# Four modulation blocks of layer 2: from TensorE products in layer 1 to VectorE multiply-adds in the scans of layer 2

## The chip, the cores and the metric

The kernel runs on one core of a Trainium2 chip. The metric is the device time of one execution in microseconds (us), lower is better. TensorE is called PE in the profile (PEld is its loading of weights), VectorE is DVE, ScalarE is ACT, GpSimd is POOL, and SyncE, which issues nearly all transfers here, is SP.

## The reference

The model is a trunk of two layers over 256 latent tokens (x) with 256 context tokens (ctx) ahead of them, 2048 features wide. Layer 1 mixes by attention (neighbourhood attention and latent attention, eight heads each). Layer 2 mixes by a gated delta rule, scanned in both directions over chunks of 64 tokens. Each layer is modulated by a conditioning vector, one for the latent tokens (c) and one for the context tokens (c_ctx):

```
def adaln_params(cond, w_mod, b_mod):
    return jnp.split(jax.nn.silu(cond) @ w_mod + b_mod, 3, axis=-1)

def deltanet_layer(x, ctx, c, c_ctx, w_mod, b_mod, norm, w_in, ..., update_ctx):
    sh, sc, gt = adaln_params(c, w_mod, b_mod)
    sh_c, sc_c, gt_c = adaln_params(c_ctx, w_mod, b_mod)
    ... modulate(x, norm, sh, sc) @ w_in ... modulate(ctx, norm, sh_c, sc_c) @ w_in ...
    x = x + gt[:, None] * deltanet_out(o_xf + flip_t(o_xb), zx, o_norm, w_out)
    if update_ctx:
        ctx = ctx + gt_c * deltanet_out(o_cf + flip_t(o_cb), zc, o_norm, w_out)
    return x, ctx
```

In layer 2, the last one, update_ctx is false. So its gate gt is needed for the latent tokens only, and only at the very end, when the output product is added to x. Shift and scale are needed for both, at the layer's beginning.

## The kernel before, in words

Everything lies feature-major: 128 features on the partitions, 16 tiles of them, and the 512 tokens (256 latent, 256 context) along the free axis. Dense products split each fp32 operand into a high and a low part of a shorter format and add three products (lines 90 to 92). A weight tile of 128 x 1024 is loaded into one of four buffers called raw, cast to its high part by ScalarE (whi) and subtracted by VectorE (wlo).

**Modulation.** The weights of a layer's modulation are 2048 x 6144. They are worked in 12 chunks of 512 columns, each 4 MB in 8 loads of 512 KB: chunks 0 to 3 are the shift, 4 to 7 the scale, 8 to 11 the gate. There are two ways to work a chunk. `adaln` (from line 121) does it on TensorE: 16 products of cond (the two samples, padded to 32 columns) with a 128 x 512 piece of weights, spread over four column groups of the array, into the tile pmod; VectorE copies that to macc; four transposes bring it to the partitions (pmt); VectorE adds the four groups and the bias into mods. A profile records each of these fp32 products as two instructions. `adaln_lanes` (from line 161) does it on VectorE: for each of 16 weight rows and each of the two samples one multiply-add `acc = raw * cond + acc` over 128 x 512 (line 177), and at the end eight products with a column of ones (line 184, tile pml) that sum over the partitions.

**Layer 1** works, in this order, the gate projection, the heads of the neighbourhood attention, the latent heads, the output product with `ab_wo`, and the norm and modulation of layer 2's input (`modulate`, lines 229 to 243, which makes the tiles hx, high and low, 16 feature tiles one after another on VectorE, ScalarE and GpSimd). The order of instructions on each engine is set there by a planner that runs the program in a simulated timeline and puts instructions where they become ready by it. Layer 2's modulation is mixed into layer 1 by generators. Chunks 0 and 1 are lanes in the neighbourhood heads. Chunks 2, 3 and 8 are products in the latent heads: `later(mr, ((1, (2, 3, 8), 0),))`, one quarter of a chunk per head, the rest after the last head. Chunk 9 follows as products behind the last head, chunks 4 to 7 are lanes in the output product, and chunks 10 and 11 are products during the norm and `modulate`. In the latent heads q's rotated part (qr) lies in a buffer that the split of the attention's output (gx, lines 502 and 503) takes over when qr has been read. cond lies with the activations of layer 1 in a pool (abx) whose space layer 2's constants (taps, ad, line 540) and pools take over.

**Layer 2** first projects gates, keys, queries, and inverts the small matrices of the delta rule. Then come the scans: a loop over steps `st` from -2 to 69, in which the order on TensorE, VectorE and ScalarE is the written order (`manual_schedule`); SP's order stays with the planner. A step is a quarter of a head. It holds a step of the context's scan C for head st // 4 and, six steps later, one of the latent tokens' scan X; in each, TensorE multiplies the state (pks, line 1033), VectorE makes R (line 1037), TensorE multiplies R into ptr (line 1045), ScalarE and VectorE split that (vh, vl), TensorE updates the state's product (line 1064) and VectorE the state (line 1073), and X ends with a product and a subtraction (lines 1078, 1083). Between these phases stand eight pieces of a value projection for later heads (`take(dn, ...)`), which keep TensorE busy, and the convolution of the values, whose taps (line 585) stand on VectorE at the middle and the end of even steps. A finished head is normed and gated (`finish`; its last instruction on VectorE, re, line 1111, ends a step with st % 4 = 0). `hi()` casts the next weight tile at the start of a step and loads ahead, so that three tiles are loaded and not yet cast; `lo()` makes the low part in the second half. From step 58 the value projection is replaced by the output product, whose `project` (line 636) reads the gate, `mods[1][:, 32 + u, 0:1]`, sample 0 alone.

`room["e"]` is a buffer of 4096 columns that the scans cut up; its last 1024 columns (`tail_e`) are used from step 56 on, for rows of the gated output read back by `gate`.

Of the kernel before, what the change touches and what calls it, by code (L numbers as in the profile page):

```python
# [16 lines left out]
KT = 16  # L17
# [9 lines left out]
def trunk_kernel(ctx: ExitStack, tc: tile.TileContext, g):  # L27
# [35 lines left out]
    ab_bmod, dn_bmod = vecs[:, 56:104], vecs[:, 104:152]  # L63
    o_gain = vecs[:, 152:153]
    mods = [cst(f"mod{l}", [128, 48, 2]) for l in range(2)]
    Am = [cst(f"Am{l}", [128, KT, 2]) for l in range(2)]


# [92 lines left out]
    def adaln_lanes(l, ps, pm, tp, chunks, after=None):  # L161

        wm, bmod, gain = ((g["ab_wm"], ab_bmod, ab_gain), (g["dn_wm"], dn_bmod, dn_gain))[l]
        for ch in chunks:
# [26 lines left out]
                V.tensor_tensor(Am[l][:, f], Am[l][:, f], gain[:, f].unsqueeze(2).broadcast_to([128, 4, 2]), op=ALU.mult)  # L191
            yield

    def steps(it, n=1000):
        for _ in range(n):
            if next(it, it) is it:
                break
# [62 lines left out]
    with tc.tile_pool(name="s0", bufs=2) as tp, tc.tile_pool(name="s0p", bufs=1, space=PSUM) as ps:  # L260
        V.memset(cond, 0.0)
        A.activation(cond[:, :, 0:2], cc, AF.Silu)
        xs = ((xA, g["xT"]), (xB, g["cT"]))
        for j in range(0, KT, 4):
            for x, src in xs:
                nc.sync.dma_start(x[:, j:j + 4], src[:, j:j + 4])

        xq = tp.tile([128, 6, 4, S], F32, name="xq", tag="zs", bufs=1)
        sums = [xq[:, 0], xq[:, 1]]
        for j in range(0, KT, 4):  # L270
            for i, (x, _) in enumerate(xs):
                sq = xq[:, i if j == 0 else 2 + (j // 2 + i) % 4]
                A.activation(sq, x[:, j:j + 4], AF.Square)
                if j > 0:
                    V.tensor_tensor(sums[i], sums[i], sq, op=ALU.add)
        for t in sums:
            V.tensor_tensor(t[:, 0:2], t[:, 0:2], t[:, 2:4], op=ALU.add)
            V.tensor_tensor(t[:, 0], t[:, 0], t[:, 1], op=ALU.add)
        rb = rstd_bcast([b for t in sums for b in blocks_of(t[:, 0], n=S)], 4, D, ps, "pz3", tp)
        rbs = tp.tile([128, T], F32, name="rbs", tag="rbs", bufs=1)  # L280
        V.tensor_copy(rbs, rb)
        pz = [ps.tile([128, T], F32, name=f"pz{i}", tag=f"pz{i}") for i in range(NP)]
        zs = tp.tile([128, NS - NP, T], F32, name="zs", tag="zs", bufs=1)

        GROUPS = [(0, 1), (1, 1), (2, 2),(4,2),(6,2), (8, 4), (12, 4)]

        def mods_of(j):
            k0, n = GROUPS[j]
            return adaln(0, ps, ("pmod", "aux"), tp, [(k0, n), (16 + k0, n)], bufs=MB)

        def modulate_of(j, r=rbs):
            k0, n = GROUPS[j]
            modulate(0, lambda k, s: (xA, xB)[s][:, k], r, hh, hl, tp, range(k0, k0 + n))

        steps(mods_of(0))
        modulate_of(0, rb)
        end = len(GROUPS) - 1
        for j, (k0, n) in enumerate(GROUPS):
            ahead = mods_of(j + 1) if j < end else iter(())
            for i in range(0, NS, 2):  # L300
                own = i < NP
                p = [pz[i + e] if own else mm_tile() for e in range(2)]
                with tc.issue_after(mod_loads[7]) if j == 0 else nullcontext():
                    sliced(wab, (i, i + 1), k0, n, hh, hl, p, not own or j == 0, not own or j == end)
                for e in range(2):
                    if not own and j == 0:
                        A.copy(zs[:, i + e - NP], p[e])
                    elif not own:
                        V.tensor_tensor(zs[:, i + e - NP], zs[:, i + e - NP], p[e], op=ALU.add)
                steps(ahead, 3)  # L310
                if i == 6 and j < end:
                    modulate_of(j + 1)
        go = [abx.tile([128, KT, S], F32, name="goA", tag="xA"), abx.tile([128, KT, S], F32, name="goB", tag="xB")]
        for j in range(NS):
            z = pz[j] if j < NP else zs[:, j - NP]
            for s in range(2):
                A.activation(go[s][:, j], z[:, s * S:(s + 1) * S], AF.Silu)

    with tc.tile_pool(name="ab", bufs=2, reuse_waits="tile") as tp, \
# [149 lines left out]
                V.tensor_tensor(ch[:, 8 + j], craw[:, j], ch[:, j].bitcast(F32), op=ALU.subtract)  # L469
        cr.release()  # L470
        mr = tc.alloc_tile_pool(name="mr2", bufs=2, reuse_waits="tile")
        ahead = later(mr, ((1, (2, 3, 8), 0),))

        rows = slice(0, 64), slice(64, 128)
        attend(*na7)
# [16 lines left out]
            attend(*o, 8 + h, None, ([qr[:, 2 * h + i] for i in range(2)], [kr[:, i] for i in range(2)]))  # L492

        steps(ahead)
        steps(later(mr, ((1, (9,), 0),), last_mm))
        pace = 0
        gx = parts_tile("gx")
        gh, gl = gx[:, 0], gx[:, 1]
# [19 lines left out]
            if j % 4 == 3:  # L518
                nc.sync.dma_start(x1d[:, j - 3:j + 1], x1[0][:, j - 3:j + 1])
        steps(ahead)  # L520
        ahead = later(mr, ((1, (10, 11), 0),), last_mm)
        rb = rstd_bcast(blocks_of(qacc, sq), 4, D, ps, "st", tp)
        hx = parts_tile("hx")
        hh, hl = hx[:, 0], hx[:, 1]
        modulate(1, lambda k, s: x1[s][:, k], rb, hh, hl, tp)
        steps(ahead)
        mr.release()

    abx.release()
# [110 lines left out]
    with tc.tile_pool(name="dn", bufs=2, reuse_waits="tile") as tp, \  # L640
# [481 lines left out]
        W += [g["dn_wo"][u][:, 1024 * c:1024 * c + 1024] for u, c in wo_order]  # L1122
        raws, wt = [], []

        def hi():
            j = len(wt)
            if j < len(W):
                while len(raws) < min(len(W), j + 3):
                    raws.append(load_raw(W[len(raws)]))
                h = wp.tile([128, 1024], F32R, name="whi", tag="whi", bufs=3)  # L1130
                A.copy(h, raws[j])  # L1131
                wt.append([h])
# [22 lines left out]
        def nothing():  # L1155
            return iter(())
# [59 lines left out]
        outs = early()  # L1216
        GATES = {56: (0, 4, 8), 57: (12, 16), 58: (20,), 66: (24,)}
        LAG = 6
        fins = nothing()
        for st in range(-2, 64 + LAG):  # L1220
            i, n = st // 4, st % 4
            j, m = (st - LAG) // 4, (st - LAG) % 4
            if n == 0 and i < 16:
                cs[i].v = v_of[i][1]
                cs[i].St = tp.tile([128, 2, 2, 128], F32, name="St", tag=("DT", "DT", "Xs")[i % 3])
                if i < 15:
                    cs[i + 1] = load(i + 1, 1)
            if m == 0:
                if -1 <= j < 15:
                    xs[j + 1] = load(j + 1, 0)  # L1230
                    xs[j + 1].v, xs[j + 1].St = v_of[j + 1][0], cs[j + 1].St
                if j >= 0:
                    xs[j].zt = zts[j % 2]
                    nc.sync.dma_start(xs[j].zt, spz[j])
                if j >= 1:
                    fins = finish(xs[j - 1])
            X = step(xs[j], m) if j >= 0 else nothing()
            C = step(cs[i], n) if 0 <= i < 16 else nothing()
            vals = st < 58
            q = (st + 2) // 2  # L1240
            if vals:
                if st % 2 == 0:
                    cur = value_unit(q)
                dn = tile_mm(cur.p, st + 2, 8 * (st % 2), hh, hl, FULL, st % 2 == 0, st % 2 == 1)
                cut = (3, 2, 3)
            else:
                dn, cut = outs, (6, 4, 6)

            if prev is not None and st % 2 == 0:
                acc = vp.tile([128, T], F32, name="acc", tag="acc")  # L1250
                x = conv_begin(prev.p, prev.ch, acc, vp.tile([128, T], F32, name="cin", tag="cin0", bufs=1))
            elif prev is not None:
                ac2 = vp.tile([128, T], F32, name="ac2", tag="ac20", bufs=1)
                tile_act(ac2, acc, AF.Silu, False)
            if m == 0:
                take(fins, 1)
            take(X, 1)
            take(C, 1)
            hi()
            take(dn, cut[0])  # L1260
            if prev is not None and st % 2 == 0:
                conv_taps(x, prev.ch, acc, (1, 3))
            if not vals:
                lo()
            if m < 2:
                take(fins, 1)
            take(X, 1)
            take(C, 1)
            if prev is not None and st % 2 == 1:
                pv = ps.tile([128, 4, 128], F32, name="pvv", tag="tr", bufs=1)  # L1270
                for b in range(4):
                    PE.transpose(pv[:, b], ac2[:, b * 128:(b + 1) * 128], ident)
                v_store(prev.kh, prev.j, pv)
                prev = None
            if m == 2:
                take(fins, 1)
            if not vals:
                hi()
            take(dn, cut[1])
            lo()  # L1280
            take(X, 1)
            take(C, 1)
            take(dn, cut[2])
            take(X, 1)
            if x is not None and prev is not None and st % 2 == 0:
                conv_taps(x, prev.ch, acc, (0, 4))
            if m == 2:
                take(fins, 1)
            if vals and st % 2 == 1:
                prev = cur  # L1290
            for k in GATES.get(st, ()):
                gate(k, 4)
            if st == 68:
                gate(28, 2, xs[14].go)
# [145 lines left out]
```

## Time and profile before

| what | value |
|---|---|
| median of 3 runs | 2491.8 us (2489.74 to 2504.61) |
| the profiled execution | 2493.04 us, its span (first to last instruction) 2491.2 us |
| PE busy | 97% of the span |
| DVE busy | 71% |
| ACT busy | 44% |
| POOL busy | 6% |
| HBM read and written | 356.94 MB and 35.39 MB, 157 GB/s over the span |
| chain that ended last, by engine | PE 88%, issue 5%, DMA 3%, DVE 2%, ACT 1% |
| granted TensorE clock, mean | 0.992 |

The profile is of one execution. A row of a group gives line, engine, operation, output<-input, shape and count, then busy time and mean duration, and after the second bar the idle time of the engine just before these instructions with what ended it. A row of the timeline gives the start in us from the span's start, the duration, engine, line, operation, tiles and count, and in brackets the idle time before it and what ended it; rows of equal kind that follow each other are merged. A row of the windows gives the stretch, its length, and for each engine the busy time and the number of instructions, then granted clock, DMA share and GB/s. The share of TensorE's busy time includes the overlap of neighbouring products, so a row can be longer than the distance to the next.

### The profile page before, as it was taken

What the parts mean: (1) busy time and instruction counts of PE and PEld (TensorE: products, weight loads), DVE (VectorE), ACT (ScalarE), POOL (GpSimd) and SP (SyncE); (2) the same over time, 40 slices, a digit from 0 to 9 for tenths busy, and PEclk for the clock granted to TensorE, in tenths of its full rate; (3) what the DMA queues carried; (4) which work ended last, traced back from release to release, by engine and by line L of the source; (5) the groups of instructions that cost most, each with busy time, mean ns of one, the idle gap of its engine ahead of it and who ended that gap; (6) DMA issues with size and microseconds to landing.
All of it is one profiled execution on the core that took longest, in us unless ns stands there. A gap on an engine that the chain in (4) does not pass through costs nothing.

```text
span 2491.2 us, 42483 instructions
## 1 busy us (share of the span) xinstructions
PE 2428.2 (97%) x16110; PEld 1963.1 (79%) x16110; DVE 1762.8 (71%) x3538; ACT 1105.6 (44%) x2446; POOL 161.1 (6%) x165
## 2 busy tenths in 40 slices
PE   6999999999989999999999999999999999999998
PEld 4557888888858878858998989987777777777787
DVE  4654678883356687856998988885777777777765
ACT  4223332333254432257565655634444544445453
POOL 0000000000000000020011101000000000012000
PEclk9999999999999999999999999999999999999999
DMA  8872645542253366664665666774343333336454
GB/s 252 282 277 87 200 154 172 169 157 84 88 187 110 102 198 204 226 210 136 195 173 158 179 178 180 204 201 108 87 116 103 115 112 98 106 100 184 148 193 141
DMA packets 254940, 397.24 MB, mean 159 GB/s; under 512 B 122257, under 2 KB 163857, under 8 KB 254609
## 3 DMA queue, kind: packets, MB, share of 16 engines
q1 hardware_dynamic: 253584, 393.00, 52.0%
q8 instruction: 127, 2.08, 0.3%
q10 hardware_dynamic: 1152, 1.54, 0.2%
q14 instruction: 77, 0.62, 0.1%
HBM read 356.94 MB, written 35.39 MB: 157 GB/s over the span
## 4 chain that ended last, share of the span: by engine, by line
PE 88%; issue 5%; DMA 3%; DVE 2%; ACT 1%; SPq 0%; POOL 0%; DVEq 0%; POOLq 0%; ACTq 0%
PE mm L90 21%; PE mm L91 20%; PE mm L92 20%; PE pks L1033 3%; PE pmod L141 3%; PE ptr L1045 2%; PE sp L365 2%; PE mm L105 2%; PE po L365 1%; DMA mraw<-dn_wm 1%; PE ptr L1078 1%; PE psu L1064 1%; PE pks L1064 1%; PE pt L398 1%; PE mm L107 1%
## 5 line engine op out<-in xcount | busy, mean ns | idle before, releaser
L90 PE MATMUL mm<-hx,whi 128*128 128x512 f32 (+1 forms) x2304 | 843.7, 366 | 2.3 <-ACT t L664 2.2
L91 PE MATMUL mm<-hx,whi 128*128 128x512 f32 (+1 forms) x2304 | 820.6, 356 | 2.5 <-issue 2.5
L92 PE MATMUL mm<-hx,wlo 128*128 128x512 f32 (+1 forms) x2304 | 819.4, 356 | 0.6 <-DVE wlo L78 0.6
L77 ACT CAST whi<-raw 128x1024 fp32r<-128x1024 f32 (+2 forms) x346 | 338.6, 980 | 701.4 <-PE mm L91 502.3
L78 DVE TENSOR_TENSOR wlo<-raw,whi 128x1024 fp32r<-128x1024 f32 (+2 forms) x346 | 394.3, 1142 | 204.3 <-ACT whi L77 198.2
L90 PEld LDWEIGHTS mm<-hx,whi 128*128 128x128 f32 x2304 | 438.8, 190 | 106.3 <-issue 27.0
L92 PEld LDWEIGHTS mm<-hx,wlo 128*128 128x128 f32 x2304 | 438.6, 190 | 65.1 <-issue 4.2
L91 PEld LDWEIGHTS mm<-hx,whi 128*128 128x128 f32 x2304 | 438.8, 190 | 61.4 <-issue 9.2
L177 DVE SCALAR_TENSOR_TENSOR lacc<-mraw,cond,lacc 128x512 f32<-128x512 f32 x300 | 208.6, 746 | 0.7 <-DMA mraw<-dn_wm 0.7
L585 DVE SCALAR_TENSOR_TENSOR acc<-cin,taps,acc 128x508 f32<-128x508 f32 (+3 forms) x256 | 187.2, 731 | 20.3 <-ACT acc L576 17.2
L105 PE MATMUL mm<-hx,whi 128*128 128x512 f32 x480 | 173.1, 404 | 0.1
L1055 DVE SCALAR_TENSOR_TENSOR vl<-ptr,egm,vh 128x128 fp32r<-128x128 f32 x224 | 64.7, 346 | 95.1 <-ACT rf L1052 37.9
L107 PE MATMUL mm<-hx,wlo 128*128 128x256 f32 x457 | 128.4, 281 | 1.3 <-DVE wlo L1139 1.2
L141 PE MATMUL pmod<-mraw,cond 128*32 128x512 f32 (+2 forms) x640 | 98.4, 508 | 28.1 <-DMA mraw<-ab_wm 18.8
L1139 DVE TENSOR_TENSOR wlo<-raw,whi 128x1024 fp32r<-128x1024 f32 x84 | 102.5, 1221 | 13.5 <-ACT whi L1131 13.4
L105 PEld LDWEIGHTS mm<-hx,whi 128*128 128x128 f32 x480 | 88.9, 188 | 24.5 <-issue 5.0
L816 DVE SCALAR_TENSOR_TENSOR outer<-L,bv,X 128x31 f32<-128x31 f32 (+15 forms) x248 | 99.4, 401 | 6.4 <-POOL X L811 0.5
L90 PE MATMUL mm<-gx,whi 128*128 128x512 f32 x256 | 100.3, 394 | 3.4 <-DVE x1B L515 2.4
L599 ACT ACTIVATE ac<-acc 128x128 f32<-128x128 f32 x160 | 37.4, 300 | 144.2 <-DVE acc L585 144.1
L91 PE MATMUL mm<-gx,whi 128*128 128x512 f32 x256 | 100.4, 392 | 0.5 <-DVE gx L503 0.5
L92 PE MATMUL mm<-gx,wlo 128*128 128x512 f32 x256 | 99.8, 391 | 0.0
L1049 ACT ACTIVATE vh<-ptr,egm 128x128 fp32r<-128x128 f32 x224 | 71.3, 374 | 57.1 <-PE ptr L1045 55.2
(301 smaller groups left out, 3648.5 us busy)
## 6 DMA issues: line engine op xcount, KB each, us to landing
raw<-dn_w SPq DMA_DIRECT2D x194, 512.0 KB
mraw<-dn_wm SPq DMA_DIRECT2D x96, 512.0 KB
mraw<-ab_wm SPq DMA_DIRECT2D x88, 512.0 KB
raw<-ab_w SPq DMA_DIRECT2D x66, 512.0 KB
raw<-dn_wo SPq DMA_DIRECT2D x64, 512.0 KB
raw<-ab_wo SPq DMA_DIRECT2D x32, 512.0 KB
raw<-ab_w SPq DMA_DIRECT2D x32, 256.0 KB
spt<-sp SPq DMA_DIRECT2D x64, 128.0 KB
```

What stands on the lines that cost most here:

```text
L77: A.copy(hi[:, :m], raw[:, :m])
L78: V.tensor_tensor(lo[:, :m], raw[:, :m], hi[:, :m].bitcast(F32), op=ALU.subtract)
L90: PE.matmul(ps, wh[:, c], xh[:, k0 + k, sl], start=first and k == 0, stop=False)
L91: PE.matmul(ps, wh[:, c], xl[:, k0 + k, sl], start=False, stop=False)
L92: end = PE.matmul(ps, wl[:, c], xh[:, k0 + k, sl], start=False, stop=last and k == kt - 1)
L105: PE.matmul(p2, wh[:, c], x[:, :, k0 + k], start=start, stop=stop)
L107: PE.matmul(p2[:, 0], wl[:, c], x[:, 0, k0 + k], start=False, stop=False)
L141: PE.matmul(pmod[32 * q:32 * q + 32, :m], cond[:, 4 * kg + q, :], raw[c // 1024][:, half + c % 1024:half + c % 1024 + m], start=kg == 0, s ...
L177: V.scalar_tensor_tensor(acc[:, s], raw[:, q], cond[:, k, s:s + 1], acc[:, s], op0=ALU.mult, op1=ALU.add)
L585: V.scalar_tensor_tensor(o3[:, :, i0:i1], p3[:, :, i0 + d:i1 + d], taps[:, ch, t:t + 1], o3[:, :, i0:i1], op0=ALU.mult, op1=ALU.add)
L816: V.scalar_tensor_tensor(o, L[:, rows, k:k + 1].broadcast_to([128, n, m]), bv[:, k:k + 1], X[:, k:k + 1, cols].broadcast_to([128, n, m]), ...
L1139: V.tensor_tensor(w, raws[j], h.bitcast(F32), op=ALU.subtract)
```

## The change

Chunks 8 to 11 of layer 2's modulation, the gate, leave layer 1. A new generator `lanes` works them in the scans, for sample 0 alone: per step one load of 512 KB (two weight rows) and two multiply-adds on VectorE, behind everything else of the step. It starts at step 4 (a load) and works a tile per step from step 5 to 36; a chunk's end (four products with ones, one addition of the bias) stands at steps 13, 21, 29 and 37, on TensorE and VectorE at the step's end. Its sums lie in two halves of the tail of `room["e"]`; its weights take the four raw buffers in turn with the value projection's tiles, which are loaded only two ahead (`depth`) while it runs. cond1 is a copy of sample 0's column of cond that outlives layer 1. The four products' output takes the PSUM buffer "tr", which the transposes of values (line 1272) and of finished heads (line 1109) use too.

```
+    cond1 = cst("cond1", [128, KT, 1])
...
+    def lanes(l, chunks, acc_of, cnd, n, pt_of):
+        wm, bmod = ((g["ab_wm"], ab_bmod), (g["dn_wm"], dn_bmod))[l]
+        tiles = [(ch, t) for ch in chunks for t in range(8)]
+        load = lambda ch, t: load_raw(wm[ch, t // 2][:, t % 2 * 1024:t % 2 * 1024 + 1024])
+        ahead = load(*tiles[0])
+        yield
+        for i, (ch, t) in enumerate(tiles):
+            raw, ahead = ahead, load(*tiles[i + 1]) if i + 1 < len(tiles) else None
+            if t == 0:
+                acc = acc_of(ch)
+            for q in range(2):
+                k = 2 * t + q
+                for e in range(n):
+                    x = raw[:, 512 * q:512 * q + 512]
+                    if k == 0:
+                        V.tensor_scalar(acc[e], x, cnd[:, k, e:e + 1], None, op0=ALU.mult)
+                    else:
+                        V.scalar_tensor_tensor(acc[e], x, cnd[:, k, e:e + 1], acc[e], op0=ALU.mult, op1=ALU.add)
+            yield
+            if t == 7:
+                pt = pt_of(n)
+                for j in range(4):
+                    for e in range(n):
+                        PE.matmul(pt[:, j, e:e + 1], acc[e][:, j * 128:j * 128 + 128], ones[:, 0:1], start=True, stop=True)
+                f = slice(4 * ch, 4 * ch + 4)
+                V.tensor_tensor(mods[l][:, f, :n], pt, bmod[:, f].unsqueeze(2).broadcast_to([128, 4, n]), op=ALU.add)
...
+        A.copy(cond1, cond[:, :, 0:1])
...
-        ahead = later(mr, ((1, (2, 3, 8), 0),))
+        ahead = later(mr, ((1, (2, 3), 0),))
...
         steps(ahead)
-        steps(later(mr, ((1, (9,), 0),), last_mm))
         pace = 0
...
         steps(ahead)
-        ahead = later(mr, ((1, (10, 11), 0),), last_mm)
         rb = rstd_bcast(blocks_of(qacc, sq), 4, D, ps, "st", tp)
...
         modulate(1, lambda k, s: x1[s][:, k], rb, hh, hl, tp)
-        steps(ahead)
...
+        depth = 3
         def hi():
             j = len(wt)
             if j < len(W):
-                while len(raws) < min(len(W), j + 3):
+                while len(raws) < min(len(W), j + depth):
...
+        gates = lanes(1, range(8, 12), lambda ch: [room["e"][:, 3072 + 512 * (ch % 2):3584 + 512 * (ch % 2)]], cond1, 1,
+                      lambda n: ps.tile([128, 4, n], F32, name="pml", tag="tr", bufs=1))
...
+            if st == 3:
+                depth = 2
+            if 4 <= st < 56:
+                depth = 2 if next(gates, 0) is None else 3
             for k in GATES.get(st, ()):
                 gate(k, 4)
```

## The prediction, made before the change was run

> **What bounds the kernel now.** I read the page first, for its span, its engines and the group of the products that go.
>
> ```profile
> span 2491.2 us, 42483 instructions
> PE 2428.2 (97%) x16110; PEld 1963.1 (79%) x16110; DVE 1762.8 (71%) x3538; ACT 1105.6 (44%) x2446; POOL 161.1 (6%) x165
> L141 PE MATMUL pmod<-mraw,cond 128*32 128x512 f32 (+2 forms) x640 | 98.4, 508 | 28.1 <-DMA mraw<-ab_wm 18.8 <-DMA mraw<-dn_wm 9.1
> ```
>
> TensorE is busy for 97% of the span. What it need not do is a gain wherever other products are ready behind it, and what makes it wait is a loss. Line 141 has 20 blocks of products; the change takes four. Next comes the view by windows, over the scan steps that take over the work:
>
> ```profile
> 1742.00:2044.00 302.00, 302.00 (x1875) 233.99 (x1874) 220.77 (x579) 143.79 (x444) 21.75 (x23) 1.00 0.36 105
> ```
>
> The columns are length, then PE, PEld, DVE, ACT and POOL, each with its count, then the clock, the DMA share and GB/s. These are steps 6 to 36 (31 in 302 us, 9.7 us each). TensorE has no gap; VectorE has 81 us, 2.6 us a step. On average 1.4 us more a step fits, but VectorE runs in a hand-written order, so what matters is where in the step the slack lies.
>
> **What is removed: the products.** The windows of the pmod tile alone (PE, PEld, DVE), where chunks 8, 9 and 10 with 11 run:
>
> ```profile
> 740.00:860.00 120.00, 6.14 (x36) 0.99 (x36) 1.38 (x2) 1.00 0.31 99
> 860.00:880.00 20.00, 7.81 (x32) 1.23 (x32) 0.69 (x1) 1.00 0.72 232
> 1066.00:1130.00 64.00, 14.61 (x64) 1.89 (x64) 1.38 (x2) 0.92 0.60 190
> ```
>
> The same for the pmt tile, the four transposes that end a chunk:
>
> ```profile
> 860.00:880.00 20.00, 0.60 (x4) 0.47 (x4) 0.00 (x0) 1.00 0.72 232
> ```
>
> A chunk has 32 recorded products. So chunk 8 takes 6.14 x 32/36 + 0.60 = 6.1 us, chunk 9 takes 8.4, and chunks 10 and 11 take 14.6 + 1.2 = 15.8: 30.3 us of TensorE in all. How much is on the path differs by place.
>
> **Chunk 8** lies among the products of the MLA heads. Its bursts displace others, but half could lie in softmax waits. Bounds 3 and 6.1; I take 6, nearest to the row.
>
> **Chunk 9** lies in the last heads' tail, where little else is ready. The timeline:
>
> ```profile
> 860.62 1.90 PE L141 MATMUL pmod<-mraw,cond 128*32 128x512 f32 x10
> 868.41 1.70 PE L141 MATMUL pmod<-mraw,cond 128*32 128x512 f32 x8
> 874.82 0.40 ACT L502 CAST gx<-goA 128x256 fp32r<-128x256 f32 x1
> 904.30 0.75 DVE L177 SCALAR_TENSOR_TENSOR lacc<-mraw,cond,lacc 128x512 f32<-128x512 f32 x1 [0.67 <-DMA mraw<-dn_wm]
> 906.65 0.77 PE L90 MATMUL mm<-gx,whi 128*128 128x512 f32 x1 [2.43 <-DVE x1B L515]
> ```
>
> The split into gx (line 502) can begin only when the last score product has read qr, since gx takes its buffer. Products of chunk 9 stand ahead of those scores, the first 1.9 us among them. Without them the split begins earlier, and the lane loads of chunk 4 need not queue behind eight loads of chunk 9; then the waits at 904 and 906 shrink (0.67 and 2.43 us). Low bound 4 (the two bursts shown, a little covered); high bound 8.4 + 0.7 + 2.4 = 11.5. I take 8, near the products' own time.
>
> **Chunks 10 and 11** lie across the start of layer 2.
>
> ```profile
> 1070.81 6.16 DMA mraw<-dn_wm
> ```
>
> ```profile
> 1077.01 1.92 PE L141 MATMUL pmod<-mraw,cond 128*32 128x512 f32 x4 [3.03 <-DMA mraw<-dn_wm]
> 1078.86 1.22 PE L90 MATMUL mm<-hx,whi 128*128 128x512 f32 x2
> 1087.69 0.69 DVE L147 COPY macc<-pmod 128x512 f32<-128x512 f32 x1 [3.85 <-PE pmod L141]
> 1105.69 1.31 POOL L243 TENSOR_TENSOR hx<-mh,hx 128x512 fp32r<-128x512 f32 x1 [2.49 <-ACT mh L241]
> 1112.69 0.33 SPq L540 DMA_DIRECT2D taps<-taps  x1
> 1112.70 0.69 DVE L147 COPY macc<-pmod 128x512 f32<-128x512 f32 x1 [8.43 <-PE pmod L141]
> 1116.32 0.39 PE L90 MATMUL mm<-hx,whi 128*128 128x256 f32 x1 [2.22 <-ACT t L664]
> ```
>
> VectorE runs in order. Its copy out of pmod waits 3.85 us for the products of chunk 10, and the normalised rows behind it wait too. So the last of them (POOL at 1105.69) would come about 4 us earlier. The second copy holds VectorE for 8.43 us. Worse, the constants of layer 2 (taps at 1112.69) load into space that cond frees, and its last reader is the last product of chunk 11; the third unit's first product at 1116.32 then waits for ScalarE, which needed them. Of the 10.6 us from 1105.69 to 1116.32 I expect 6 to go. Together 10. Low bound 3.85, the first wait alone; high bound 15.8, all the products' time. I take 10 because both waits are rows and the early bursts, before 1078.86, fill a gap.
>
> The row of the clock there is
>
> ```profile
> 1070.00:1080.00 10.00, 6.97 (x22) 2.24 (x18) 5.85 (x14) 5.41 (x14) 3.32 (x3) 0.67 0.68 212
> ```
>
> with a granted clock of 0.67 after waits. [...]
>
> Sum of what goes: 6 + 8 + 10 = **24 us** (bounds 11 and 33).
>
> **What is added, in the scans.** Per chunk 8 loads, 15 multiply-adds and one multiply, four products with ones, and one addition of the bias. The nearest rows are layer 1's own lanes, and as a piece of the chain the 8 products that end one of its chunks, which has two samples:
>
> ```profile
> 1048.79 1.41 DVE L177 SCALAR_TENSOR_TENSOR lacc<-mraw,cond,lacc 128x512 f32<-128x512 f32 x2
> ```
>
> ```profile
> 1066.05 1.79 PE pml L184 x16
> ```
>
> So each of 32 steps (5 to 36) gets 1.41 us of VectorE, and four steps get half of 1.79, 0.9 us of TensorE: 3.6 us, fully on the path. The bias additions wait for those; behind them on VectorE stand the next chunk's first two instructions and the R of an even step, which has slack (below). The copy to cond1 at the start is nothing: ScalarE is idle 56% of the time.
>
> The multiply-adds stand last in the step, behind the taps, ahead of the next step's R, for which TensorE's ptr products wait. Into an odd step:
>
> ```profile
> 1851.40 0.75 DVE L1111 SCALAR_TENSOR_TENSOR re<-pot,ngain,re 128x512 f32<-128x512 f32 x1
> 1852.06 0.60 DVE L1037 SCALAR_TENSOR_TENSOR R<-pks,neg,vx 128x128 f32<-128x128 f32 x2
> 1852.58 0.60 DVE L1037 SCALAR_TENSOR_TENSOR R<-pks,neg,vc 128x128 f32<-128x128 f32 x2
> 1853.14 0.60 PE L1045 MATMUL ptr<-R,rb 128*128 128x128 f32 x4
> 1853.58 0.61 PE L1045 MATMUL ptr<-R,ra 128*128 128x128 f32 x4
> ...
> 1871.24 0.60 DVE L1037 SCALAR_TENSOR_TENSOR R<-pks,neg,vc 128x128 f32<-128x128 f32 x2
> 1872.90 0.61 PE L1045 MATMUL ptr<-R,ra 128*128 128x128 f32 x4
> ```
>
> R for the second head is whole at 1853.18; with 1.41 more, 1854.59. Its second product, 0.22 after 1853.58, needs it at 1853.80: **0.8 us late**. That is the odd step behind one that ends a head (re). In the other kind, 1871.84 + 1.41 = 1873.25 against 1873.12: **0.13 late**. Into an even step:
>
> ```profile
> 1859.31 0.42 DVE L1083 TENSOR_TENSOR rf<-rf,ptr 128x256 f32<-128x256 f32 x1 [1.07 <-PE ptr L1078]
> 1860.34 0.61 DVE L1037 SCALAR_TENSOR_TENSOR R<-pks,neg,ra 128x128 f32<-128x128 f32 x2 [0.60 <-PE pks L1033]
> 1860.86 0.60 DVE L1037 SCALAR_TENSOR_TENSOR R<-pks,neg,vc 128x128 f32<-128x128 f32 x2
> 1861.38 0.74 DVE L585 SCALAR_TENSOR_TENSOR acc<-cin,taps,acc 128x510 f32<-128x510 f32 x1
> 1861.57 1.14 POOL L1016 TENSOR_TENSOR ksp<-rf,ksp 128x256 fp32r<-128x256 f32 x1 [19.74 <-ACT ksp L1015]
> 1862.15 1.11 DVE L585 SCALAR_TENSOR_TENSOR acc<-cin,taps,acc 128x510 f32<-128x510 f32 x1
> 1862.82 0.60 PE L1045 MATMUL ptr<-R,re 128*128 128x128 f32 x4
> ```
>
> R began 0.61 after rf ended, so it slips 0.8, the second head's end to 1862.26, still ahead of 1862.82: nothing. Sum 8 x 0.8 + 8 x 0.13 = 7.4, with the products **11 us**. If all is absorbed 2 us remain; with taps and later work also late, 20.
>
> The 32 loads leave SP's queue of layer 1 and join it in the scans, where weight tiles share their four buffers. A weight load now starts at the end of the split two steps before its use:
>
> ```profile
> 1876.42 0.34 SPq L71 DMA_DIRECT2D raw<-dn_w  x1
> 1891.39 1.03 ACT L1131 CAST whi<-raw 128x1024 fp32r<-128x1024 f32 x1
> ```
>
> Those 15 us stand against the 6.16 us that a load of the same size took above under heavier traffic, and the DMA share in the scans is 0.36. Costed at nothing; if that cover went, ScalarE's cast would stop, and with it everything behind it on ScalarE. The gate rows' load into the same buffer tail now waits for step 37; it is used at step 56.
>
> **The sum.** The profiled execution took 2493.04 us (span 2491.2 and 1.8 around it): 2493.0 - 24 + 11 = 2480.0. The median of the runs is 1.2 lower, so **2479 us**, 13 below the median. The likeliest case reaches from 2467 to 2491.
>
> **Rivals.**
>
> *More is freed at layer 2's start.* With the high bounds in layer 1 (33) and half of the R waits in the scans (3.7 + 3.6 = 7): 2491.8 - 26 = 2466. For it speaks that VectorE, SP and TensorE all stand at 1112.7 behind one chunk; against it that the rows' own pace stays.
>
> *The products were filler.* Low bounds (11) and 11 in the scans: 2492, no change. For it speak the gaps at 1077 and 860 to 877; against it the 8.43 us wait.
>
> *VectorE sets the step.* If no slack takes the additions, because R heads a loop in which each step's late end delays the next, 32 x 1.41 + 3.6 = 49 us is added: 2491.8 - 24 + 49 = 2517, slower. It decides from (24 - 3.6)/32 = 0.64 us lost per step. For it speaks the 0.8 above; against it the 0.6 us that VectorE idles before even steps' R.
>
> *GpSimd's key split collides.* The tap at 1862.15 took 1.11 us beside POOL's 1.14, the tap before it 0.74. If all 16 key splits (one at each even step) hold a multiply-add for their 1.1 us and it lands on the path, 18 us more: 2497. [...]
>
> **How the numbers follow.** Forecast 0.55, more freed 0.18, filler 0.14, VectorE sets the step 0.08, key split 0.05. About 1% (25 us) is what a measurement of this kernel can tell. Faster by over 1% is the first rival and the lower edge of the forecast, 0.20; slower by over 1% is most of the third rival, 0.06; the rest is 0.74. The range runs from a little under the first rival, 2463, to the fourth, 2497.
>
> **What would show it.** Right: line 141 has 512 products; the third unit's first product follows the last row of hx by some 4 us instead of 10.6; in steps 5 to 36 TensorE waits for R at odd steps only, under 1 us, in turn large and small; no ScalarE cast waits for raw. Wrong: R waits at every step, casts that wait for DMA, or a layer 1 that is shorter by less than 15 us.

## The result and the profile after

The changed kernel takes a median of 2513.45 us (2510.53 to 2517.49, six runs); the kernel before, on the same chip, 2492.09 us (2489.74 to 2504.61, six runs). The ratio is 1.0077, with a 95% interval of 1.0058 to 1.0097: the change costs some 21 us, where 13 us less was forecast. The line numbers after are 1 higher in the early helpers, 30 or 31 higher in layer 1 and 28 or more higher in the scans. From the page of the changed kernel, the span, the busy time of the engines, and the group of the modulation's products on TensorE:

```profile
span 2512.0 us, 42324 instructions
PE 2425.9 (97%) x15998; PEld 1973.2 (79%) x15998; DVE 1799.6 (72%) x3594; ACT 1106.9 (44%) x2447; POOL 159.8 (6%) x165
L142 PE MATMUL pmod<-mraw,cond 128*32 128x256 f32 (+2 forms) x512 | 71.0, 477 | 26.7 <-DMA mraw<-ab_wm 18.9
```

The 128 recorded products are gone, 27.4 us of them. The span grew by 20.8 us, and it grew at two places. VectorE began the last normed tile of layer 2's input (mh, from which the last row of hx is made) at 1103.40 before and begins it at 1109.87: by there the kernel is 6.5 us late, where the prediction's terms had it 18 early. 3.2 us of that are recovered before the scans; the scans then add 17.0.

**First place: the latent heads.** The windows from 740 to 880 us (PE, PEld, DVE, ACT, POOL, clock, DMA share, GB/s), of before:

```profile
740.00:880.00 140.00, 140.00 (x790) 110.32 (x789) 87.28 (x192) 65.28 (x153) 0.00 (x0) 1.00 0.37 118
```

and of after, first all instructions, then those of the tile lacc alone, the lanes' multiply-adds with the products that end them:

```profile
740.00:880.00 140.00, 131.07 (x709) 109.53 (x708) 130.17 (x263) 58.85 (x130) 0.00 (x0) 0.98 0.45 142
```

```profile
740.00:880.00 140.00, 3.80 (x32) 4.04 (x32) 63.36 (x91) 0.98 0.45 142
```

Before, 68 of TensorE's 790 records there were pmod's and 12 the transposes pmt; after, 4 and 4, and 32 end the lanes. So the heads' own products fell from 710 to 669 in the same time, although 64 records of pmod had made room. VectorE went from 87 to 130 us, and 63 us of that are lanes of chunks 4 to 7, none of which ran there before. The change does not touch their code. One chain of the timeline after, across the end of that window, shows what they do in the heads; the waits of TensorE in the window (engine, tile, line, releaser: us, times, longest) stand below it:

```profile
878.74 0.86 PE L396 MATMUL sp<-kr,cx 128*128 128x512 f32 x3
879.45 0.73 DVE L178 SCALAR_TENSOR_TENSOR lacc<-mraw,cond,lacc 128x512 f32<-128x512 f32 x1
...
880.38 1.40 DVE L178 SCALAR_TENSOR_TENSOR lacc<-mraw,cond,lacc 128x512 f32<-128x512 f32 x2
881.70 1.20 DVE L79 TENSOR_TENSOR wlo<-raw,whi 128x1024 fp32r<-128x1024 f32 x1
882.83 0.67 DVE L420 TENSOR_REDUCE mx<-sp 128x1 f32<-128x512 f32 x1
883.54 0.69 ACT L423 ACTIVATE pr<-sp,mx 128x512 f32<-128x512 f32 x1 [0.47 <-DVE mx L420]
884.37 0.62 PE L396 MATMUL sp<-kT,qT 128*128 128x256 f32 x3 [1.49 <-ACT pr L423]
```

```profile
PE sp L396 <- ACT pr L423: 4.4, 3, 1.7
PE mm L91 <- DVE qT L392: 1.5, 4, 0.7
```

The scores (sp) are complete at 879.60. Three multiply-adds, 2.13 us, a scaling and a weight split stand on VectorE ahead of their row maximum (mx), which begins at 882.83. The exponential on ScalarE (pr) waits for that maximum, and TensorE's next scores wait 1.49 us for ScalarE. In the window no wait of TensorE, VectorE or ScalarE is ended by a load, so the higher DMA share (0.45 against 0.37) is not what stops them.

**Second place: the scans.** The same stretch of 31 steps whose window stands in the prediction, after:

```profile
1745.25:2062.50 317.25, 313.29 (x1900) 239.34 (x1899) 262.95 (x644) 145.25 (x444) 18.82 (x23) 1.00 0.53 150
```

It took 302.0 us and takes 317.3. The cast of a step's weight tile marks the steps. Before, over the 34 steps that hold everything added:

```profile
1745.00 1.05 ACT L1131 CAST whi<-raw 128x1024 fp32r<-128x1024 f32 x1
...
2074.81 1.06 ACT L1131 CAST whi<-raw 128x1024 fp32r<-128x1024 f32 x1
```

and after:

```profile
1748.26 1.05 ACT L1162 CAST whi<-raw 128x1024 fp32r<-128x1024 f32 x1
...
2095.06 1.06 ACT L1162 CAST whi<-raw 128x1024 fp32r<-128x1024 f32 x1
```

329.81 us became 346.80: 17.0 more. Behind the last of these the two kernels run at the same pace.

### The profile page after: what moved, and what is told of

Same layout as the page of the kernel before. It is cut to its first block, busy times and chain, and to the rows that moved or that the text cites. A ratio compares the mean times of both kernels' runs of the same rounds, so it can differ in the third digit from the quotient of the medians.

```text
span 2512.0 us, 42324 instructions
## 1 busy us (share of the span) xinstructions
PE 2425.9 (97%) x15998; PEld 1973.2 (79%) x15998; DVE 1799.6 (72%) x3594; ACT 1106.9 (44%) x2447; POOL 159.8 (6%) x165
## 4 chain that ended last, share of the span: by engine, by line
PE 81%; DVE 8%; issue 6%; DMA 3%; ACT 2%; SPq 0%; POOL 0%; DVEq 0%; POOLq 0%; ACTq 0%
PE mm L91 20%; PE mm L92 19%; PE mm L93 19%; PE pks L1061 3%; PE ptr L1073 2%; PE pmod L142 2%; PE mm L106 2%; PE sp L396 1%; DVE wlo L79 1%; DVE acc L613 1%; PE ptr L1106 1%; DVE lacc L178 1%; PE po L396 1%; PE psu L1092 1%; PE mm L108 1%
## 5 line engine op out<-in xcount | busy, mean ns | idle before, releaser
L340 DVE TENSOR_TENSOR zs<-zs,mm 128x512 f32<-128x512 f32 x72 | 49.2, 686 | 69.0 <-PE mm L93 68.8
L142 PE MATMUL pmod<-mraw,cond 128*32 128x256 f32 (+2 forms) x512 | 71.0, 477 | 26.7 <-DMA mraw<-ab_wm 18.9
```

Source lines behind the costliest of these rows:

```text
L142: PE.matmul(pmod[32 * q:32 * q + 32, :m], cond[:, 4 * kg + q, :], raw[c // 1024][:, half + c % 1024:half + c % 1024 + m], start=kg == 0, s ...
```

## The experiments

**Theory of the dam.** Before, the lanes of chunks 4 to 7 came after chunk 9 in the same ring of buffers (mraw), and chunk 9's products are queued behind the last unit of the last head. So chunk 9 kept the lanes out of the heads without anyone having written that down: `issue_after(last_mm)` around the lanes' own loads binds instructions on TensorE only, and there is none inside: in the changed kernel the lanes begin at 750, long before the product that it names. Without chunk 9 the planner puts the lanes where their weights are ready by its timeline, into the heads. **Rivals:** the products were filler, and the lanes play no part; or chunk 9's going had another cost. For the scans: the place of the multiply-adds counts (they stand ahead of an odd step's R), against their amount.

### Layer 1 alone, with and without a hold

The first kernel is before without chunks 8 to 11, and nothing in the scans. It leaves the gate out (its rows are set to zero), as do the kernels below that leave out chunks without working them elsewhere:

```
+    V.memset(mods[1][:, 32:48], 0.0)
...
-        ahead = later(mr, ((1, (2, 3, 8), 0),))
+        ahead = later(mr, ((1, (2, 3), 0),))
...
-        steps(later(mr, ((1, (9,), 0),), last_mm))
...
-        ahead = later(mr, ((1, (10, 11), 0),), last_mm)
...
-        steps(ahead)
```

> Layer 1 of the change alone: chunks 8 to 11 are left out of layer 1 and not computed anywhere (the gate rows are zero). The prediction's sum: 24 us less than before, about 2468. Theory of the dam (chunks 8 and 9 kept the lane multiply-adds of chunks 4 to 7 out of the latent heads; without them VectorE runs those beside the softmax, and TensorE waits for it): about 3 us more than before, some 2495, with the lane multiply-adds between 750 and 936 us as in the changed kernel. Rival, the products were filler: no change, 2492, with the lane multiply-adds playing no part.

Measured: 2495.58 us against 2490.41 (ratio 1.0015, 1.0002 to 1.0029). Taking 27 us of work off TensorE gains nothing.

The second has in addition the hold, on VectorE this time: attend returns its last instruction there, and in adaln_lanes the multiply-adds stand under the order, where only the loads stood.

```
+                    nc.sync.dma_start(raw, wm[ch, kg].rearrange("p (q c) -> p q c", q=4)[:, 2 * i:2 * i + 2])
                     with tc.issue_after(after) if after else nullcontext():
-                        nc.sync.dma_start(raw, wm[ch, kg].rearrange("p (q c) -> p q c", q=4)[:, 2 * i:2 * i + 2])
...
+                        for q in range(2):
+                            k = 4 * kg + 2 * i + q
+                            for s in range(2):
...
-            attend(*o, 8 + h, None, ...)
+            last_go = attend(*o, 8 + h, None, ...)
...
-                ahead, pace = later(mr, ((1, (4, 5, 6, 7), 1),), last_mm), 1
+                ahead, pace = later(mr, ((1, (4, 5, 6, 7), 1),), last_go), 1
```

> As the run without chunks 8 to 11, but the lane multiply-adds of chunks 4 to 7 are queued on VectorE behind the last gating of the last head, so they cannot run among the heads. Theory of the dam: the whole predicted saving is there, 24 us less than before, about 2468, and TensorE has no gap from 740 to 860 us. Rival, the products were filler: within 5 us of the run without the hold, so 2490 to 2500.

Measured: 2473.45 us (0.9923, 0.9902 to 0.9944), 17 us less than before and 22 less than without the hold. Its window:

```profile
740.00:880.00 140.00, 138.97 (x774) 117.45 (x771) 94.72 (x212) 72.17 (x173) 0.00 (x0) 1.00 0.22 69
```

TensorE is all but full again, with VectorE at 95 us. The lanes' place was the loss; that the products were filler falls for the heads. Of the 24 us forecast, 17 came.

### The dam by itself

Three kernels look at the dam from other sides: before without chunk 9 alone; before with all its work and without the order for chunk 9; and before with the hold.

```
-        steps(later(mr, ((1, (9,), 0),), last_mm))
...
-        steps(later(mr, ((1, (9,), 0),), last_mm))
+        steps(later(mr, ((1, (9,), 0),)))
```

> Before with chunk 9 alone left out (its gate rows are zero). The prediction's term: 8 us less, 2484. Theory of the dam: chunk 8 still stands in the ring, and by the written order one chunk of the lanes in place of three moves ahead of the splits into gx; a third of the 27 us lost in the changed kernel, so 8 won and 9 lost: 2493, no change.

Measured: 2509.24 us against 2490.41 (1.0067, 1.0047 to 1.0086), 19 us more. The dam's sign was right and its size was not: not 9 us were lost but some 24 (against the 2485.07 of the same work with the hold, below). The lanes begin here at 800, when chunk 8 is done, and 64 multiply-adds run before the first split into gx, against 96 in the changed kernel. Its window shows the same loss:

```profile
740.00:880.00 140.00, 131.63 (x715) 106.84 (x714) 109.54 (x223) 57.09 (x125) 0.00 (x0) 0.98 0.42 139
```

> Before, nothing left out; only the instruction order that holds chunk 9's products behind the last latent head's unit is taken away, so that chunk 9, and in the ring behind it the lanes of chunks 4 to 7, may run earlier. Theory of the dam: by the written order about two chunks of the lanes move ahead of the splits into gx, and the kernel becomes 10 to 25 us slower, 2500 to 2515, though no work is added. Rival, what the kernel without chunk 9 lost had another cause: no change, 2490.

Measured: 2505.64 us against 2490.60 (1.0059, 1.0043 to 1.0075). One argument less in one call, the same work, and the kernel is 15 us slower, with 25 multiply-adds ahead of the splits. Chunk 9's own products run earlier here as well, so not all of the 15 need be the lanes'.

> Control: before with all its chunks, and the lane multiply-adds of chunks 4 to 7 queued behind the last gating of the last head. Theory of the dam: before has the dam already, so the hold brings nothing: 2490, within 4 us. Rival, the hold is a gain of its own, and the 17 us of the runs with it are its work and not that of the chunks left out: 2475 to 2480.

Measured: 2496.97 us against 2492.01 (1.0018, 1.0005 to 1.0031). The hold is no gain by itself; it costs 5 us where chunk 9 still dams. So the 17 us come from the chunks left out. Whether those 5 us are also paid where the chunks are gone was not separated: against this kernel in place of before, leaving them out is worth some 22.

The loss against the same work with the hold is 22 us for 96 early multiply-adds (2495.58 - 2473.45), 24 us for 64 (2509.24 against 2485.07, below) and 9 us for 25 (2505.64 - 2496.97). It does not go with their number; what each costs at which softmax was not separated.

### The terms of layer 1 one by one

Before with the hold and without chunk 9; the same without 8 and 9; and before, unheld, without 10 and 11.

> Before with the hold, and chunk 9 alone left out (its gate rows are zero). The prediction's term for chunk 9: 8 us less, 2482. From the time that the whole layer 1 saved with the hold (17 in place of 24): 5 to 6 us less, 2485. Without the hold the same kernel took 19 us more than before.

Measured: 2485.07 us (0.9967, 0.9956 to 0.9978), 6.9 less than before, and 11.9 less than the kernel above with the hold alone.

> Before with the hold, and chunks 8 and 9 left out (their gate rows are zero). The prediction's terms: 6 + 8 = 14 us less, 2476. From the last residual row of the run without all four chunks (11 us earlier than before): 2479.

Measured: 2479.27 us (0.9953, 0.9936 to 0.9969), 12.7 less. Chunk 8 is worth 5.8.

> Before with chunks 10 and 11 left out (their gate rows are zero), chunks 8 and 9 in place, so with the dam. The prediction's term: 10 us less, 2480. From the start of layer 2 in the run without all four chunks: 6 to 9 us less, 2481 to 2484.

Measured: 2492.03 against 2492.01 us (1.0003, 0.9990 to 1.0016): nothing. The expected waits do go. In the timeline without chunks 10 and 11 the last row of hx is ready at 1101.60, and then:

```profile
1107.19 0.58 PE L91 MATMUL mm<-hx,whi 128*128 128x256 f32 x1 [3.04 <-ACT t L663]
...
1119.36 1.12 PE L674 MATMUL pb<-ident,ac 128*128 128x128 f32 x4 [3.48 <-ACT ac L595]
1120.53 0.80 PE L91 MATMUL mm<-hx,whi 128*128 128x512 f32 x1
1121.13 0.63 PE L92 MATMUL mm<-hx,whi 128*128 128x512 f32 x1
```

The row of hx is 4.1 us earlier than before and the third unit's first product 9.1 (1107.19 against 1116.32). Then a wait for ScalarE, 0.75 before, takes 3.48, and the products of 512 columns behind it last 0.80 and 0.63 us, where the first such before last 0.40 and 0.39: the transposes into pb are only 4.0 earlier (before 1123.37), and the first vh of the scans 2.2. In the key stage between, this kernel lost 2 us more; its written order there differs from before, and which instruction loses them stays open.

### The scan part alone, and its place in the step

Layer 1 as before with all chunks, and the change's scans (chunks 8 to 11 are worked twice):

> The scan part of the change alone: layer 1 as before with all its chunks, and chunks 8 to 11 worked out a second time in the scans as the change does it (the second result is the one used). The prediction: 11 us more, 2503. As the changed kernel's steps read: 17 us more, 2509 (8 heads by 1.7 and 4 chunks by 0.8). Rival, VectorE sets the step: 49 us more, 2541.

Measured: 2506.98 us against 2490.41 (1.0062, 1.0043 to 1.0081), 16.6 more. With the 5 of layer 1 alone this makes the 21 of the whole change.

Then the changed kernel with the multiply-adds of an even step moved to the odd one, behind the phase that makes R:

```
             take(X, 1)
             take(C, 1)
+            if 4 <= st < 56 and st % 2 == 1:
+                next(gates, 0)
             hi()
...
-            if 4 <= st < 56:
+            if 4 <= st < 56 and st % 2 == 1:
                 depth = 2 if next(gates, 0) is None else 3
```

> The changed kernel with the gates' multiply-adds moved inside the scans: two tiles in each odd step and none in an even one, the first right behind R, the second at the step's end. Theory: the 13.8 us of the scans beyond the products with ones come from two multiply-adds that stand ahead of an odd step's R; behind R they fit into the 1.6 to 1.8 us in which VectorE waits for ScalarE's vh. So 2513 - 13 = 2500, and TensorE's waits for R at odd steps are gone. Rival, the amount of VectorE's work counts and not its place: no change, 2513.

Measured: 2498.65 us against 2490.60 (1.0033, 1.0024 to 1.0043); the changed kernel had 1.0077. The casts of the same steps:

```profile
1745.49 1.05 ACT L1162 CAST whi<-raw 128x1024 fp32r<-128x1024 f32 x1
...
2078.46 1.06 ACT L1162 CAST whi<-raw 128x1024 fp32r<-128x1024 f32 x1
```

332.97 us: 3.2 more than before instead of 17.0, with the same instructions. In an odd step:

```profile
1872.52 0.60 DVE L1065 SCALAR_TENSOR_TENSOR R<-pks,neg,vc 128x128 f32<-128x128 f32 x2
1873.03 1.53 DVE L214 SCALAR_TENSOR_TENSOR re<-raw,cond,re 128x512 f32<-128x512 f32 x2
1873.73 0.60 PE L1073 MATMUL ptr<-R,re 128*128 128x128 f32 x4
1874.48 0.68 DVE L1132 TENSOR_TENSOR rf<-rf,rn 128x512 f32<-128x512 f32 x1
1875.36 1.14 DVE L1083 SCALAR_TENSOR_TENSOR vl<-ptr,egm,vh 128x128 fp32r<-128x128 f32 x4 [0.19 <-ACT rh L1080]
```

The pair runs while TensorE multiplies R and ScalarE makes vh; VectorE still waits 0.19 us before vl. With the amount unchanged, the place made the difference.

### Both repairs

> The changed kernel with the lane multiply-adds of chunks 4 to 7 queued on VectorE behind the last gating of the last head. By the parts measured so far: 17 us saved in layer 1 and 17 added in the scans, 2490, no change against before. The prediction's sum would have it at 2479.

Measured: 2489.90 us against 2490.60 (0.9993, 0.9983 to 1.0002).

> Both repairs together: the lanes of chunks 4 to 7 held behind the last head, the gates' multiply-adds in odd steps alone. By the parts: 2490 - 17 + 3 to 4 for the products with ones = 2477, faster than both kernels. Rival, as the prediction has it, SP's queue and depth 2 cost nothing but more traffic: 2485 to 2490.

Measured: 2473.65 us against 2490.60 (0.9938, 0.9921 to 0.9954): 17 us faster than before and 40 faster than the changed kernel, with all of the work done. From its page:

```profile
span 2471.6 us, 42331 instructions
PE 2404.8 (97%) x15998; PEld 1962.6 (79%) x15998; DVE 1805.4 (73%) x3594; ACT 1106.2 (45%) x2447; POOL 159.5 (6%) x165
```

The work is the changed kernel's, and VectorE's busy time is within 6 us of it; order alone separates the two.

## Why the prediction was wrong

**The step that failed** is chunk 9: "Without them the split begins earlier, and the lane loads of chunk 4 need not queue behind eight loads of chunk 9", counted as 8 us won. That the lanes would start earlier was right, and it was the loss: they went as far ahead as the planner could put them, into stretches where VectorE carries the softmax. The split into gx began 12.7 us later (887.48 against 874.82), not earlier. Without the hold the chunk's going costs 19 us; with it the kernel gains 6.9 against before (11.9 against the hold alone). The prediction listed what would be freed and did not ask what the freed order would start next.

**Chunk 8**, 6 us: 5.8 with the hold. Right.

**Chunks 10 and 11**, 10 us: nothing alone, about 4 behind the other two (12.7 against 17.0 less, in two sets of runs). The step to the last row (4 us) and the one to the third unit's product (5.6 us behind that row, forecast "some 4") were right; what was left out is that ScalarE sets the next steps there (TensorE waits 3.04 and 3.48 us for it), and gives the lead back. For these two chunks alone, then, the rival of the filler held. Without these products the granted clock from 1070 to 1080 is lower, 0.56 where it was 0.67:

```profile
1070.00:1080.00 10.00, 5.34 (x18) 3.98 (x18) 5.72 (x15) 5.11 (x13) 3.29 (x3) 0.56 0.18 52
```

The last row of hx still comes 4.1 us earlier behind this window. Where the lead is lost, the clock was 0.84 and 0.70 in the two windows of 10 us from 1110 to 1130, and 0.88 and 0.95 before; what of the loss is the clock and what the waits was not separated.

**What layer 1 gives** is then 17 us and not 24 where the order is kept, inside the bounds of 11 to 33, and -5 where it is not, which no bound held.

**The scans**, 11 us: 17.0. The products with ones are the term of 3.6, and 3.2 is what the kernel with the multiply-adds behind R still loses. R late, 7.4, was then 13.8. The prediction's two kinds of odd step, after:

```profile
1859.87 1.53 DVE L214 SCALAR_TENSOR_TENSOR re<-raw,cond,re 128x512 f32<-128x512 f32 x2
1861.32 0.60 DVE L1065 SCALAR_TENSOR_TENSOR R<-pks,neg,vx 128x128 f32<-128x128 f32 x2
1861.72 0.75 PE L1073 MATMUL ptr<-R,rb 128*128 128x128 f32 x4 [0.62 <-DVE R L1065]
1862.30 0.68 PE L1073 MATMUL ptr<-R,ra 128*128 128x128 f32 x4
...
1881.41 0.75 PE L1073 MATMUL ptr<-R,re 128*128 128x128 f32 x4
1881.71 0.62 ACT L1069 ACTIVATE rf<-pks,neg 128x128 f32<-128x128 f32 x2 [1.06 <-DVE R L1065]
1882.22 1.04 ACT L1162 CAST whi<-raw 128x1024 fp32r<-128x1024 f32 x1
1883.16 0.64 ACT L1077 ACTIVATE vh<-ptr,egm 128x128 fp32r<-128x128 f32 x2
1884.42 0.38 PE L1092 MATMUL psu<-vh,ksp 64*128 64x256 f32 x1
1884.85 0.35 PE L1092 MATMUL ptr<-vh,ksp 64*128 64x256 f32 x1
```

Set against the same instructions of before, the lag grows in the step behind re from 7.81 us to 8.58 at the first product of R (1861.72 against 1853.14) and to 8.80 behind the second: 0.77 and 0.22, where 0.8 was forecast. In the other kind it grows from 8.84 to 8.95 (1881.41 against 1872.46) and to 9.17: 0.11 and 0.22, where 0.13 was forecast. There 0.50 us come on top, up to 9.65 behind the state's products, that the prediction did not have. By the waits of the profile: ScalarE's rf stands behind R, the cast and vh stand behind rf, and the state's products wait for vh. Before, the same rows of ScalarE and the first of the state's products were

```profile
1871.72 0.60 ACT L1041 ACTIVATE rf<-pks,neg 128x128 f32<-128x128 f32 x2
1873.16 0.63 ACT L1049 ACTIVATE vh<-ptr,egm 128x128 fp32r<-128x128 f32 x2
1875.27 0.38 PE L1064 MATMUL psu<-vh,ksp 64*128 64x256 f32 x1
```

so that ScalarE is 10.0 us late here where TensorE's products of R are 8.95. In all that is 1.82 a head, and 13.8 over eight heads is 1.73. The list of who waits for R had only TensorE on it. Even steps cost nothing, as forecast.

**The loads** at depth 2 cost nothing: no ScalarE cast waits for raw in the scans, at a DMA share of 0.53. **GpSimd's key split** runs beside eight of the pairs, each ahead of an even step's R. They took 2.04 or 2.05 us and every other pair of multiply-adds 1.53, and it costs nothing. One of the eight:

```profile
1888.98 2.05 DVE L214 SCALAR_TENSOR_TENSOR re<-raw,cond,re 128x512 f32<-128x512 f32 x2
```

2.05 us in place of 1.53, with a subtraction of 0.74 us on GpSimd beside it from 1889.74; TensorE lags by 9.65 us ahead of this pair and behind it. **VectorE sets the step**, the slower rival, had a time near the one measured (2517) by luck and not its mechanism: it put 49 us into the scans, where 17 came, and kept the 24 won in layer 1.

Of the signs named ahead for being right, the 512 products, the waits for R at odd steps only (none over 1.0 us) and the casts that never wait for raw came true, and the third unit's first product follows the last row of hx by 5.6 us. Of those for being wrong one came true, a layer 1 shorter by less than 15 us: it was longer.

## What to carry to other kernels

Before taking work out of a schedule that a planner fills, ask what the work was holding back: a ring of buffers and an order given for one part can keep a later part in its place, and if that place matters it must be written for that part itself, on the engine that does its work. Added work in a fixed order goes where its engine waits for another one, and not at the end of a step: list every engine that waits for the next instruction behind it, and count the slip of each. A saving at the head of a stage is measured at the stage's end.

## What the runs showed of the hardware

In the changed kernel's heads TensorE's granted clock fell to 0.50 behind four waits of at most 1.45 us:

```profile
851.24 0.50 PE L396 MATMUL sp<-kT,qT 128*128 128x512 f32 x1 [1.45 <-ACT kT L388]
851.99 0.63 PE L429 MATMUL pt<-ident,pr 128*128 128x128 f32 x4 [0.26 <-DVE vt L389]
853.29 0.58 PE L396 MATMUL po<-PT,vt 128*128 128x256 f32 x1 [0.68 <-ACT PT L388]
854.81 0.80 PE L91 MATMUL mm<-cx,whi 128*128 128x512 f32 x1 [0.26 <-DVE qT L392]
855.40 0.63 PE L92 MATMUL mm<-cx,whi 128*128 128x512 f32 x1
855.83 0.63 PE L93 MATMUL mm<-cx,wlo 128*128 128x512 f32 x1
```

Four waits, 2.65 us in the 5.0 us from 849.8 to 854.8 and none longer than 1.45. The granted clock was 1.00 until 852, 0.73 from 852 to 854 and 0.50 from 854 to 858, and the products behind the waits run 0.43 us apart in place of 0.23 until 859.7, 4.9 us long. More was lost in the heads than the length of the waits: from 740 to 880 us the changed kernel's TensorE idles 8.9 us and spends 3.8 on the products that end the lanes, and it runs 41 of the heads' products fewer, although some 13 us of pmod are gone from there. Not every such cluster does it: waits of 1.65, 0.25 and 0.24 us between 826.5 and 831.6 left the clock at 1.00, and the products from 831.62 to 834.24 run 0.23 to 0.33 us apart. What decides stays open.
